# A transformer block on one core: product 6's results are added in two groups, GpSimd subtracts U from another sum, and the last stores are queued earlier

## The chip, the core and the metric

The kernel runs on one core of a Trainium2 chip. The time is the device time of one execution in microseconds (us); three executions are shown, and their median counts. Besides the times there is one profiled execution with its trace. Its engines are called PE (TensorE, matmuls; PEld is its loading of weights), DVE (VectorE), ACT (ScalarE), POOL (GpSimd) and SP (SyncE, which here only issues DMAs). Each engine works through its instructions in the order in which the program gave them to it. POOL cannot read PSUM, the memory into which matmuls write; DVE and ACT can.

## What is computed

One layer on 512 tokens of width 2048: attention of two kinds and a convolution, an output projection, and then a feed-forward part (SwiGLU) with 5632 hidden channels. The change touches only the feed-forward part:

```
h2 = _rms_norm(x, norm2_g[l])
x = x + (jax.nn.silu(h2 @ w_gate[l]) * (h2 @ w_up[l])) @ w_down[l]
```

## The kernel before

**Seven products for eight.** In the feed-forward part every matrix product is cut into 2x2 quarters and computed with seven products of quarters instead of eight (a scheme of Strassen's kind). Each product adds its result to, or subtracts it from, one or more of four sums, which are called (i, k) with i and k 0 or 1; each sum is held in two tiles, a = 0 and a = 1, of 128 x 512. The products come in the order 7, 1, 4, 6, 5, 2, 3 (`ORDER`). Product 7 goes into (1,1), 1 into (0,0), 4 into (1,0), 6 is added to (0,1) and subtracted from (1,0) and (1,1), 5 is subtracted from (1,1), 2 goes into (0,0) and 3 into (0,1). The banks are started anew in products 7, 1, 5 and 2; in 4, 6 and 3 the matmuls go on adding to what the banks hold from the product before the last. So the bank that product 6 leaves holds a term named U, which goes into three sums.

**Up and Down.** `Up` computes gate and up weights, in 11 blocks of two halves each; a half is one pass through the seven products. `Down` computes the down weights in 12 blocks d0 to d11. A Down block covers one of six ranges of pairs of hidden tiles, 4, 3, 4, 3, 4 and 4 pairs long (`RANGES`), and one of two groups g of output channels. The blocks of the ranges with three pairs are d2, d3, d6 and d7. d10 is the last block of g = 1, d11 the last of all, of g = 0.

**Units.** Each product takes two units of weights, c = 0 (A) and c = 1 (B). A unit is a tile of 128 x 1024, two pairs, and in the ranges of three pairs the second unit has one pair, 128 x 512. A weight is used as a high and a low part, so every product of two tiles is three matmuls: high by high, high weight by low activation, low weight by high activation. The high part, `wh`, and a copy of it in PSUM, `wn` (`near` in the code), are made by ACT (L268, L269), and the low part, `wl`, by DVE (L270), which subtracts `wn` from the raw weight. A unit is split two units before it is used (`SPLIT_AHEAD`). The raw weight tiles are called 11, 12, 21, 22 and s, with A or B for the unit; product 7 uses s, 1 uses 11, 4 uses 22, 6 uses 11, 5 uses 21, 2 uses 12 and 3 uses 11 again, which POOL has added to other raw tiles in between (L171).

**The order of the work.** Two lists order what goes along with the matmuls. `evacs` runs ahead of each unit, `extras` behind it, one entry of each per unit: `later(n, ...)` puts a call into entry n, counted from the next run on, so `later(0, ...)` means one unit later. Ahead of each unit stand, in this order, POOL's additions of raw weights, the entry of `evacs`, and the splitting of the unit two ahead. A product writes two of four banks, one for each a, and the product after the next writes the same two again. When a product has been issued it queues `done`, so its banks are read in the first unit of the next product. Product 6 is thus evacuated at the first unit of product 5, ahead of the splitting of 12A; at the second unit 12B is split; at the first unit of product 2 product 5's banks are read and 11A is split.

In Up, `done` reads each of product 6's banks three times on DVE (L1221 to L1223; in the first half ACT makes the first copy for a = 0). In Down (L1455 to L1460), ACT copies each bank into a slot `u` (L1457), POOL subtracts that from (1,1) one or two units later (L1458, done at L1442, the line that every addition in Down has), and DVE subtracts the bank from (1,0) and adds it to (0,1). Product 5 is subtracted from (1,1) by DVE.

**The end.** The sums of Down are turned back with DVE transpositions (`turn_back`, L1349) into buffers `z` and stored by `put` (L1359), four DMAs on SP for each pair of tiles (i, k). In d10 `done` of product 3 queues the eight transpositions and four stores of g = 1 (L1476 to L1480); they run along with d11. The order is (0,0), (1,1), (1,0), (0,1). In d11, which has `self.end`, (1,0) and (1,1) are turned back after products 6 and 5 (L1472 to L1475), and the last product, 3, has a tail of its own (`if tail`): both units are taken first, with no entry of `extras` run; then (0,0) is stored, half of (0,1), and the other half of (0,1), turned on PE, is stored from tiles `end` (L1419). What is left in `evacs` and `extras` runs after that (L1486).

Of the kernel before, what the change touches and what calls it, by code (L numbers as in the profile page):

```python
# [115 lines left out]
def kernel(ctx: ExitStack, tc: tile.TileContext, xT, wi, wo, wgu, wd, cst_in, outT):  # L116
    nc = tc.nc
# [19 lines left out]
    def slot(name, dt=F32, cols=T):  # L137
        return sp.tile([P, cols], dt, name=name, tag="s")

    def bank(name, cols=T, pool="banks"):  # L140
        return psum[pool].tile([P, cols], F32, name=name, tag="b")
# [187 lines left out]
    b = bank("idle")  # L329
    for i in range(WARM):  # L330
        nc.tensor.matmul(b, idle, idle[:, None, :].to_broadcast([P, NT, P]), start=True, stop=True)
    b = idle = None
# [146 lines left out]
    def project(name):  # L479
        b = bank(name, pool="tiles")  # L480
        for half in range(2):
            wh, wl = next_unit()
            for kk in range(8):
                k = 8 * half + kk
                s = slice(kk * P, (kk + 1) * P)
                mm3(b, wh[:, s], wl[:, s], h_hi[k], h_lo[k], k == 0, k == KT - 1)
                if kk == 3:
                    lows_now()
                if kk % 2 == 1:
                    ticks.tick()  # L490
        return b
# [445 lines left out]
    for name in PROJ[HEAD4:]:  # L937
# [4 lines left out]
        b = project(name)  # L942
# [17 lines left out]
    b = box = boxes = shared = None  # L960
# [81 lines left out]
    for half in range(2):  # L1042
        for i, n in enumerate(OUT_ORDER[half]):
            if half == 1 and i == 2:
                open_banks(banks=2, high=2)
            b = bank(f"o{half}_{n}", pool="tiles")
            wh, wl = next_unit()
            for kk in range(8):
                k = 8 * half + kk
# [18 lines left out]
    b = m_hi = m_lo = r1b = mult_a = bias_a = bias_c = over = upper = None  # L1068
# [17 lines left out]
    evacs, extras = [], []  # L1086
# [15 lines left out]
    def later(n, fn, *args, queue=evacs):  # L1102
        while len(queue) <= n:
            queue.append([])
        queue[n].append((fn, *args))
# [59 lines left out]
    class Up:  # L1165
# [39 lines left out]
        def less(self, k, a, b):  # L1205
            t = self.c[1, k, a]
            nc.vector.tensor_sub(t, t, b)

        def done(self, first, q, banks):
            if first and q == 7:  # L1210
                self.c = {}
            by = self.keep if first else self.add
            for a, b in enumerate(banks):
                if q == 7:
                    by(1, 1, a, b)
                elif q == 1:
                    by(0, 0, a, b)
                elif q == 4:
                    by(1, 0, a, b)
                elif q == 6:  # L1220
                    by(0, 1, a, b)  # L1221
                    self.less(0, a, b)
                    self.less(1, a, b)  # L1223
                elif q == 5:
                    self.less(1, a, b)
                else:
                    self.add(0, q - 2, a, b)
            if first:
                return
            if q in (6, 5):  # L1230
                later(1, self.gate, 6 - q, queue=extras)
            elif q == 2:
                self.dram = tc.dram_tile([T, T], F32, name=f"bd{self.n}")
            if q in (2, 3):
                later(0, self.weigh, q - 2)
                later(2, self.turn, q - 2)
                later(3, self.store, q - 2, queue=extras)
            if q == 3:
                first, every = (34, 20) if self.n == NBLOCKS - 1 else (5, 13)
                for at in range(2):  # L1240
                    later(first + every * at, Pair, self.dram, 2 * self.n + at, at, queue=extras)
# [120 lines left out]
    class Down:  # L1362
# [81 lines left out]
        def less(self, i, k, a, src, eng=nc.vector):  # L1444
            self.add(i, k, a, src, eng, "tensor_sub")

        def done(self, q, banks):
            for a, b in enumerate(banks):
                if q == 7:
                    self.add(1, 1, a, b)  # L1450
                elif q == 1:
                    self.add(0, 0, a, b)
                elif q == 4:
                    self.add(1, 0, a, b)
                elif q == 6:  # L1455
                    u = slot(f"d{self.t}u{a}")
                    nc.scalar.copy(u, b)  # L1457
                    later(a, self.less, 1, 1, a, u, nc.gpsimd)  # L1458
                    self.less(1, 0, a, b)
                    self.add(0, 1, a, b)  # L1460
                elif q == 5:
                    self.less(1, 1, a, b)
                    if self.end:
                        self.add(0, 1, a, b)
                elif q == 2 and self.end:

                    t = slot(f"last{a}")
                    nc.scalar.copy(t, b)
                    self.add(0, 0, a, t, nc.gpsimd)
                else:  # L1470
                    self.add(0, q - 2, a, b)
            if self.end and q in (6, 5):  # L1472
                for a in range(2):
                    later(a, turn_back, self.sum(1, int(q == 5), a))
                later(2, put, self.g, 1, int(q == 5))  # L1475
            if q == 3 and self.final:  # L1476
                for n, (i, k) in enumerate(((0, 0), (1, 1), (1, 0), (0, 1))):
                    for a in range(2):
                        later(4 + 2 * n + a, turn_back, self.sum(i, k, a))
                    later(2 * n + 6, put, self.g, i, k, queue=extras)  # L1480

    for t in range(len(DOWN)):
        blk = Down(t)
# [87 lines left out]
```

## Time and profile before

| | |
|---|---|
| median of three executions | 1861.2 us (1860.76 to 1861.59) |
| the profiled execution's own time | 1860.95 us |
| its span, from its first to its last instruction | 1859.2 us |
| PE busy | 1842.0 us, 99% of the span |
| DVE, ACT, POOL busy | 77%, 71%, 55% |
| mean granted PE clock | 0.998 |

The rows of the profile are read like this. In the timeline: start in us from the span's beginning, duration, engine, line, operation, output<-inputs, shapes, count; in brackets the idle time of the engine before it and what ended that. Several alike in a row are merged, with their count. In the view of waits: who waited, for whom, us in total, times, longest. In the groups of DMA issues: count, size of one, median us from issue to landing. The releaser of a wait is inferred; a row that names an engine which had been done long before means another one.

### The profile page before, as it was taken

How to read it: one execution, taken by the hardware profiler on the slowest of the kernel's cores; microseconds unless marked ns; L12 is line 12 of the kernel's file. 1: busy time of each engine (PE TensorE's matmuls, PEld its weight loads, DVE VectorE, ACT ScalarE, POOL GpSimd, SP SyncE). 2: the span in 40 equal slices, each digit the busy share in tenths (PEclk: the TensorE clock that was granted, in tenths of full speed). 3: DMA queues.
4: the chain of work that ended last, by engine and by line, in shares of the span. 5: the costliest groups of instructions: out<-in, count | busy, mean ns of one | idle time of the engine just before them, and what ended most of it. 6: DMA issues, size and time to landing. Idle time of an engine off the chain costs nothing.

```text
span 1859.2 us, 26562 instructions
## 1 busy us (share of the span) xinstructions
PE 1842.0 (99%) x8370; PEld 1526.1 (82%) x8370; DVE 1434.4 (77%) x2054; ACT 1320.6 (71%) x1794; POOL 1013.9 (55%) x778
## 2 busy tenths in 40 slices
PE   9999999999999999999999999999999999999997
PEld 7888888888888888888888888888887887888886
DVE  6778878998689777777777777777777777777776
ACT  6355644553468778888888888878877877877774
POOL 0135533110003567776778768868768658755552
PEclk9999999999999999999999999999999999999999
DMA  7242243333343366777767876777689768767545
GB/s 274 76 147 90 77 139 105 95 123 128 131 136 107 110 163 178 209 213 179 221 185 195 222 192 192 210 191 216 177 263 314 254 210 277 249 217 237 175 141 91
DMA packets 382987, 330.36 MB, mean 178 GB/s; under 512 B 171648, under 2 KB 311552, under 8 KB 382848
## 3 DMA queue, kind: packets, MB, share of 16 engines
q1 hardware_dynamic: 382704, 328.66, 59.8%
q8 instruction: 67, 1.10, 0.2%
q14 instruction: 72, 0.59, 0.1%
q10 hardware_dynamic: 144, 0.01, 0.0%
HBM read 255.56 MB, written 64.63 MB: 172 GB/s over the span
## 4 chain that ended last, share of the span: by engine, by line
PE 95%; DVE 1%; POOL 1%; ACT 1%; issue 1%; DMA 1%; SPq 0%; DVEq 0%; ACTq 0%; POOLq 0%
PE out L1183 15%; PE out L1181 15%; PE out L1184 15%; PE out L1433 6%; PE out L1434 6%; PE out L1432 6%; PE o L309 3%; PE o L307 3%; PE o L308 3%; PE cq L307 2%; PE cq L308 2%; PE cq L309 2%; PE ak L307 1%; PE aq L307 1%; PE av L307 1%
## 5 line engine op out<-in xcount | busy, mean ns | idle before, releaser
L1183 PE MATMUL out<-wl,h 128*128 128x512 f32 x1232 | 479.4, 389 | 0.5 <-DVE wl L270 0.5
L1181 PE MATMUL out<-wh,h 128*128 128x512 f32 x1232 | 479.4, 389 | 0.0
L1184 PE MATMUL out<-wh,h 128*128 128x512 f32 x1232 | 479.3, 389 | 0.0
L1183 PEld LDWEIGHTS out<-wl,h 128*128 128x128 f32 x1232 | 231.2, 188 | 49.0 <-DVE wl L270 0.9
L1184 PEld LDWEIGHTS out<-wh,h 128*128 128x128 f32 x1232 | 231.2, 188 | 48.1
L1181 PEld LDWEIGHTS out<-wh,h 128*128 128x128 f32 x1232 | 231.2, 188 | 47.8
L1433 PE MATMUL out<-wl,a 128*128 128x512 f32 x620 | 241.4, 389 | 5.3 <-DVE wl L270 5.3
L1434 PE MATMUL out<-wh,a 128*128 128x512 f32 x620 | 240.5, 388 | 0.0
L1432 PE MATMUL out<-wh,a 128*128 128x512 f32 x620 | 240.4, 388 | 0.0
L274 ACT CAST wh<-w 128x1024 fp32r<-128x1024 f32 (+2 forms) x94 | 96.8, 1031 | 153.6 <-PE o L308 64.5
L1442 DVE TENSOR_TENSOR y<-y,out 128x512 f32<-128x512 f32 x190 | 126.4, 684 | 65.6 <-PE out L1434 39.0
L252 DVE TENSOR_TENSOR wl<-w,wh 128x1024 fp32r<-128x1024 f32 (+2 forms) x95 | 113.3, 1192 | 41.7 <-ACT wh L274 40.1
L1433 PEld LDWEIGHTS out<-wl,a 128*128 128x128 f32 x620 | 116.4, 188 | 32.6 <-DVE wl L270 8.7
L1432 PEld LDWEIGHTS out<-wh,a 128*128 128x128 f32 x620 | 116.4, 188 | 24.1 <-ACT wh L269 0.2
L1434 PEld LDWEIGHTS out<-wh,a 128*128 128x128 f32 x620 | 116.4, 188 | 23.5
L518 DVE SCALAR_TENSOR_TENSOR y<-bu,cst,y 128x511 f32<-128x511 f32 (+14 forms) x120 | 89.8, 748 | 0.7
L307 PE MATMUL o<-mh_c,wh 128*128 128x512 f32 x128 | 51.1, 399 | 0.0
L307 PE MATMUL cq<-hh,wh 128*128 128x512 f32 x128 | 50.5, 395 | 0.0
L309 PE MATMUL o<-mh_c,wl 128*128 128x512 f32 x128 | 50.0, 391 | 0.0
L308 PE MATMUL cq<-hl,wh 128*128 128x512 f32 x128 | 49.9, 390 | 0.0
L308 PE MATMUL o<-ml_c,wh 128*128 128x512 f32 x128 | 49.9, 390 | 0.0
L309 PE MATMUL cq<-hh,wl 128*128 128x512 f32 x128 | 49.9, 390 | 0.0
(2364 smaller groups left out, 4771.6 us busy)
## 6 DMA issues: line engine op xcount, KB each, us to landing
od<-a SPq DMA_DIRECT2D x154, 256.0 KB, 4.4
a<-od SPq DMA_DIRECT2D x154, 256.0 KB, 5.7
w<-in_wi SPq DMA_DIRECT2D x58, 512.0 KB, 3.4
w<-in_wo SPq DMA_DIRECT2D x32, 512.0 KB, 3.3
x<-in_xT SPq DMA_DIRECT2D x16, 256.0 KB, 7.0
xr<-in_xT SPq DMA_DIRECT2D x16, 256.0 KB, 3.7
x2d<-xr SPq DMA_DIRECT2D x16, 256.0 KB, 2.0
z<-x2d SPq DMA_DIRECT2D x64, 64.0 KB, 3.9
```

The lines of the kernel that those rows point to most:

```text
L252: fn(*args)
L274: (nc.vector.tensor_copy if u == 0 else nc.scalar.copy)(hi[:, :n], t[:, :n])
L307: nc.tensor.matmul(out, wh, xh, start=start, stop=False)
L308: nc.tensor.matmul(out, wh, xl, start=False, stop=False)
L309: nc.tensor.matmul(out, wl, xh, start=False, stop=stop)
L1181: nc.tensor.matmul(b, x[:, high], wh[:, s], start=c == f == 0 and q in (7, 1, 5, 2), stop=False, skip_group_check=True)
L1183: nc.tensor.matmul(b, x[:, high], wl[:, s], start=False, stop=False, skip_group_check=True)
L1184: nc.tensor.matmul(b, x[:, low], wh[:, s], start=False, stop=c == f == 1, skip_group_check=True)
L1432: nc.tensor.matmul(b[:, lo:hi], x[:, high], wh[:, s], start=start, stop=False, skip_group_check=True)
L1433: nc.tensor.matmul(b[:, lo:hi], x[:, high], wl[:, s], start=False, stop=False, skip_group_check=True)
L1434: nc.tensor.matmul(b[:, lo:hi], x[:, low], wh[:, s], start=False, stop=last, skip_group_check=True)
L1442: getattr(eng, op)(t, t, src)
```

## The change

- In Up, product 6's three operations on the bank a = 1 are queued one unit later than those on a = 0 (`six`).
- In Down the same, and their content is arranged anew. DVE subtracts the bank from (1,1) and adds it to (0,1). In d11 DVE also subtracts it from (1,0); elsewhere ACT copies the bank into `u` after that, and POOL subtracts `u` from (1,0) one unit later.
- In d11 the store of (1,0) is queued in `extras`, at the same entry number, and that of (1,1) one entry of `evacs` earlier.
- In d10 the transpositions and stores of g = 1 are queued in earlier entries: the transpositions of a = 0 at 2, 3, 6, 7 instead of 4, 6, 8, 10, and the stores at 4, 5, 8, 9 instead of 6, 8, 10, 12.

```diff
+        def six(self, by, a, b):
+            by(0, 1, a, b)
+            self.less(0, a, b)
+            self.less(1, a, b)
+
...
                 elif q == 6:
-                    by(0, 1, a, b)
-                    self.less(0, a, b)
-                    self.less(1, a, b)
+                    if a:
+                        later(0, self.six, by, a, b)
+                    else:
+                        self.six(by, a, b)
...
+        def six(self, a, b):
+            self.less(1, 1, a, b)
+            self.add(0, 1, a, b)
+            if self.end:
+                self.less(1, 0, a, b)
+            else:
+                u = slot(f"d{self.t}u{a}")
+                nc.scalar.copy(u, b)
+                later(0, self.less, 1, 0, a, u, nc.gpsimd)
+
...
                 elif q == 6:
-                    u = slot(f"d{self.t}u{a}")
-                    nc.scalar.copy(u, b)
-                    later(a, self.less, 1, 1, a, u, nc.gpsimd)
-                    self.less(1, 0, a, b)
-                    self.add(0, 1, a, b)
+                    if a:
+                        later(0, self.six, a, b)
+                    else:
+                        self.six(a, b)
...
             if self.end and q in (6, 5):
                 for a in range(2):
                     later(a, turn_back, self.sum(1, int(q == 5), a))
-                later(2, put, self.g, 1, int(q == 5))
+                later(2 if q == 6 else 1, put, self.g, 1, int(q == 5), queue=extras if q == 6 else evacs)
             if q == 3 and self.final:
                 for n, (i, k) in enumerate(((0, 0), (1, 1), (1, 0), (0, 1))):
                     for a in range(2):
-                        later(4 + 2 * n + a, turn_back, self.sum(i, k, a))
-                    later(2 * n + 6, put, self.g, i, k, queue=extras)
+                        later((2, 3, 6, 7)[n] + a, turn_back, self.sum(i, k, a))
+                    later((4, 5, 8, 9)[n], put, self.g, i, k, queue=extras)
```

## The prediction

> **What bounds the kernel.** I read the page first, then who waited for whom on PE, then the order of time around those waits, then the queue of stores at the end.
>
> ```profile
> span 1859.2 us, 26562 instructions
> ...
> PE 1842.0 (99%) x8370; PEld 1526.1 (82%) x8370; DVE 1434.4 (77%) x2054; ACT 1320.6 (71%) x1794; POOL 1013.9 (55%) x778
> ```
>
> PE is the bound: its matmuls are untouched by the change, so no more can be won than the 17 us (1859.2 - 1842.0) in which it isn't busy. The waits of PE over the whole run, and then of 1500 to 1700 us alone:
>
> ```profile
> PE out L1433 <- DVE wl L270: 5.3, 6, 1.4
> ...
> PE out L1183 <- DVE wl L270: 0.5, 1, 0.5
> ```
> ```profile
> PE out L1433 <- DVE wl L270: 4.3, 4, 1.4
> ```
>
> PE waits for nothing but wl, the low part of a split weight block. Four of the waits lie in 1500 to 1700 us: one in each of the four blocks of three pairs (d2, d3, d6, d7); the two others are in d0. The wait in d6, on PE:
>
> ```profile
> 1659.68 0.39 PE L1434 MATMUL out<-wh,a 128*128 128x512 f32 x1
> 1659.91 0.39 PE L1432 MATMUL out<-wh,a 128*128 128x512 f32 x1
> 1661.27 0.50 PE L1433 MATMUL out<-wl,a 128*128 128x512 f32 x1 [0.97 <-DVE wl L270]
> 1661.61 0.40 PE L1434 MATMUL out<-wh,a 128*128 128x512 f32 x1
> ```
>
> Matmuls start every 0.23 us, so this one came 1.13 us late (1.36 - 0.23), and the next lost another 0.11 (0.34 - 0.23). The profile books only 0.97, because it lets a matmul end 0.39 us after its start. The four waits thus cost about 4.3 + 4 x 0.16 + 4 x 0.11 = 5.4 us. What made wl late, on the other engines:
>
> ```profile
> 1651.27 1.27 ACT L1457 COPY d6u<-out 128x512 f32<-128x512 f32 x2
> 1651.89 2.48 DVE L1442 TENSOR_TENSOR y<-y,out 128x512 f32<-128x512 f32 x4 [0.77 <-ACT d6u L1457]
> ...
> 1652.43 1.02 ACT L268 CAST wn<-w('12', 'd6A')_15933 128x1024 fp32r<-128x1024 f32 x1
> ...
> 1654.28 1.22 DVE L270 TENSOR_TENSOR wl<-w('12', 'd6A')_15933,wn 128x1024 fp32r<-128x1024 f32 x1
> 1654.33 0.59 ACT L268 CAST wn<-w('12', 'd6B')_15955 128x512 fp32r<-128x512 f32 x1
> 1654.85 0.62 ACT L269 CAST wh<-w('12', 'd6B')_15955 128x512 fp32r<-128x512 f32 x1
> 1655.41 0.68 DVE L270 TENSOR_TENSOR wl<-w('12', 'd6B')_15955,wn 128x512 fp32r<-128x512 f32 x1
> ...
> 1656.01 0.68 DVE L1442 TENSOR_TENSOR y<-y,out 128x512 f32<-128x512 f32 x1
> 1656.54 1.05 ACT L269 CAST wh<-w('11', 'd6A')_15783 128x1024 fp32r<-128x1024 f32 x1
> ...
> 1658.08 1.28 POOL L1442 TENSOR_TENSOR y<-y,d6u 128x512 f32<-128x512 f32 x1
> ...
> 1659.40 0.69 DVE L1442 TENSOR_TENSOR y<-y,out 128x512 f32<-128x512 f32 x1 [2.70 <-PE out L1434]
> 1660.00 1.21 DVE L270 TENSOR_TENSOR wl<-w('11', 'd6A')_15783,wn 128x1024 fp32r<-128x1024 f32 x1
> ```
>
> DVE stood idle for 2.70 us before product 5's second subtraction. The row names PE, but product 5 had ended 18 matmuls before 1659.91, at 1655.8; what ended at 1659.36 is POOL's subtraction of U from the same sum, (1,1). DVE works in order, so wl of 11A, wanted by PE from 1660.1, stood behind it. Over the run:
>
> ```profile
> DVE y L1442 <- POOL y L1442: 15.5, 8, 2.7
> ```
>
> **The change, part by part.** *Down, which sum POOL subtracts from.* DVE now takes product 6 from (1,1) itself, and POOL takes U from (1,0), which nobody touches for the next fourteen products. POOL still does two operations a block, DVE four, ACT two copies: no work is added, and DVE's wait for POOL goes.
>
> That doesn't yet free PE, because the order is new. ACT's copy of a bank now follows DVE's two operations on it, and the second bank comes one unit later, behind wl of 12A. Do the two readers of one bank wait for each other? In the fence above DVE began at 1651.89, when the copy begun at 1651.27 had run its 0.6 us; over the run DVE so waited in all twelve blocks:
>
> ```profile
> who waited for it (us, times):
> ...
>   DVE y L1442: 10.0, 12
> ```
>
> I take the reverse order to wait as well, though no row here has it. The Trainium skill (PSUM — Partial Sum Buffer, "PSUM bank collisions raise a hardware error") says that two engines must not be in one bank at once, reads against reads included. By that rule the copy has to wait; without it, the sum would be that of the first rival below, so the rule speaks against the change.
>
> d6 again, with these durations (successors on an engine start 0.1 before the end shown, a hand-over costs 0.04). Bank 0 is complete at 1651.25: DVE's two operations 1651.29 to 1652.58, copy to 1653.21, near of 12A 1653.11 to 1654.13, wl of 12A 1654.17 to 1655.39 (0.1 earlier than before). Behind it bank 1's two, 1655.30 to 1656.59; copy to 1657.21; near and wh of 12B to 1657.70 and 1658.25; wl of 12B to 1658.42; product 5's two operations, no longer waiting, to 1659.62; wl of 11A 1659.53 to 1660.75, before 1661.21. **So wl comes 0.46 earlier where 1.13 was wanted.** What is late next is wh of 11A (near from 1658.18, wh to 1660.2 against PE at 1659.91). Bank 1 is free at 1657.25; product 2 wants it at about 1657.2 (1659.91 less twelve matmuls), so there is no margin there, and I cost it at 0 to 0.1. Three blocks give 0.46; in d3 the wait was 1.4 instead of 1.0 because DVE's start hung on a late copy, and it now leads, so 0.9. **Sum 2.3 us**, between 0 (hand-overs longer than 0.04) and 5.4 (no wait between readers). Blocks of four pairs have 1.4 us more in product 5 and in product 2 each, and of DVE's work nothing more but 0.5 in the second unit; their covers hold. The two waits in d0, 1.0 booked (5.3 - 4.3), I leave as they are; they are neither in the sum nor in its bounds, and would add up to that if the new order took them too.
>
> *Up, product 6's six operations in two groups of three.* The one wait of PE (0.5 booked, about 0.8 by spacing as above) is here:
>
> ```profile
> 1405.38 0.75 DVE L1203 SCALAR_TENSOR_TENSOR b10c<-out,n2r,b10c 128x512 f32<-128x512 f32 x1
> ...
> 1407.23 0.75 DVE L1203 SCALAR_TENSOR_TENSOR b10c<-out,n2r,b10c 128x512 f32<-128x512 f32 x1
> 1407.89 1.28 DVE L1207 TENSOR_TENSOR b10c<-b10c,out 128x512 f32<-128x512 f32 x2
> 1409.08 1.22 DVE L270 TENSOR_TENSOR wl<-w('12', 'u21A')_13542,wn 128x1024 fp32r<-128x1024 f32 x1
> ```
>
> wl of 12A moves up from 1409.08 to 1407.23, so the wait goes; bank 1's three then end about 1410.4 instead of 1409.2, and the gate on ACT with them. Between 0.8 (kept) and 0 (the DMA-fed start of Down eats it) I take 0.4. The other 21 half-blocks show no wait of PE, hence nothing to win.
>
> *The end.* g = 1's eight transpositions move from runs 5 to 12 of the last block to runs 3 to 9. Its last store was queued in extras at 12, but the tail's units run no extras, so it went out last of all:
>
> ```profile
> 1844.91 7.61 SPq L1359 DMA_DIRECT2D out_T<-z  x12
> 1852.62 0.88 SPq L1419 DMA_DIRECT2D out_T<-end  x2
> 1853.56 2.33 SPq L1359 DMA_DIRECT2D out_T<-z  x4
> ```
> ```profile
> out_T<-z SPq DMA_DIRECT2D x4, 128.0 KB, 2.8
> out_T<-end SPq DMA_DIRECT2D x2, 128.0 KB, 1.8
> ```
>
> The last four issues end at 1855.9 and the last begins some 0.6 earlier, so it lands near 1858.1, 1.1 before the span's end. Without them the last is end's second, issued about 1853.1, landing near 1854.9: **3.2 us**. Those four issues and their 512 KB move to run 9, about 1834, where SP waits for DVE. The rest of SP's row is one backlog from 1844.91, so what starts it counts. That is DVE:
>
> ```profile
> 1830.56 2.64 DVE L1442 TENSOR_TENSOR y<-y,out 128x512 f32<-128x512 f32 x4 [0.31 <-ACT d11u L1457]
> ...
> 1837.79 2.44 DVE L1442 TENSOR_TENSOR y<-y,out 128x512 f32<-128x512 f32 x4
> 1840.15 1.21 DVE L270 TENSOR_TENSOR wl<-w('11', 'd11A')_17315,wn 128x1024 fp32r<-128x1024 f32 x1
> ...
> 1842.49 1.18 DVE L270 TENSOR_TENSOR wl<-w('11', 'd11B')_17338,wn 128x1024 fp32r<-128x1024 f32 x1
> 1843.60 1.88 DVE L1349 STREAM_TRANSPOSE z<-y 128x512 f32<-128x512 f32 x3
> ```
>
> In the last block DVE takes two operations from POOL (+1.2 us) and one transposition of run 8 to 11 moves ahead (three of g = 1 there instead of four, -0.6). So wl of 11A ends 0.6 later, at 1842.0, and wl of 11B, with one transposition fewer ahead of it, again at 1843.7. The tail's first wl is wanted no earlier than 1842.2: hidden, by 0.2; if that cover goes, PE loses up to 0.4. At 1843.60 the first transposition is now (1,1)'s own, so its store starts 0.6 before 1844.91. **3.2 + 0.6 = 3.8 us**, between 2.6 (0.6 lost instead) and 5.8 (SP never late: end's copies are done by 1850.1, the two issues begin at once, 2.0 more).
>
> **Sum:** 2.3 + 0.4 + 3.8 = 6.5 us off the profiled execution's 1860.95, which has 1.75 around its span of 1859.2. The median shown is 1861.2, 0.25 above it: **1854.7**.
>
> **Rivals.** *Readers don't wait for each other.* Then ACT copies at once, wl of 11A in d6 is early, and all 5.4 go: 1854.7 - 3.1 = 1851.6. For it: I have no row of a copy behind DVE. Against: the twelve waits of the other order.
>
> *The waits only move.* Hand-overs cost as much as POOL's wait did, Down's start eats the 0.8, the last block loses its 0.2 of cover: 2.6 left, 1858.6, which a measurement can hardly tell from no change (0.2% is 3.7 us). For it: margins of 0 to 0.2 in d6 and the last block.
>
> *Slower: 12A's near copy is late.* Bank 1's operations now stand behind wl of 12A, and that waits for ACT:
>
> ```profile
> DVE wl L270 <- ACT wn L268: 70.3, 89, 3.4
> ```
>
> In the three-pair blocks every us of such lateness goes to PE; from 6.5 / 4 = 1.6 us in each it decides. With the longest wait, 3.4, in all four: 1854.7 + 13.6 = 1868.3. Against: near of 12A started right behind the copies in d6. Up has about 3 us of margin (8.2 from bank 0's end to product 2's second bank, 36 matmuls, against 5.0 of DVE's work).
>
> *It doesn't do what it says* can't be: (1,0) gets nothing after product 6, so the new subtraction can't be waited for.
>
> **Numbers.** Forecast 64%, readers parallel 16%, waits only move 11%, slower 9%. The range 1850.8 to 1858.0 takes in the first two and leaves most of the others, two in ten, out. Faster by over 0.2%, 0.81; within, 0.11; slower, 0.08.
>
> **What will show it.** DVE's wait for POOL on y vanishes; PE's wait for wl in 1500 to 1700 us falls from 4.3 to about 2, and in the three-pair blocks stands behind wh and wl of 11A; L1183's wait is gone; SP's last row is end's two, and the span ends near 1853. Wrong it would be if DVE waits for 12A's near copy in these blocks, or if PE waits for a bank in product 2.

## The result, and the profile after

The changed kernel takes 1853.23 us (median of six executions, 1851.97 to 1854.6), beside 1861.09 us for the kernel before in the same series (six, 1859.25 to 1861.59): a ratio of 0.996 with a 95% interval of 0.9947 to 0.9973. The forecast was 1854.7 us. The profiled execution took 1853.5 us, 7.4 less than the 1860.95 of before; the sum forecast for it was 6.5.

The page of the changed kernel, span and busy time:

```profile
span 1851.8 us, 26509 instructions
## 1 busy us (share of the span) xinstructions
PE 1842.3 (99%) x8370; PEld 1525.9 (82%) x8370; DVE 1436.4 (78%) x2056; ACT 1317.2 (71%) x1792; POOL 1012.6 (55%) x776
```

PE looks as busy as before (1842.0), though its work is the same and the span 7.4 us shorter. That is the modelled end of a matmul: a start up to 0.16 us late is booked as busy, as the prediction noted, and behind a late start even more (in the rows of d6 below 0.37 us stand without a bracket, since the matmul before is shown 0.50 us long). The view of PE's waits in the changed kernel must be read with that in mind:

```profile
PE idle L331 <- DVE ones L341: 1.1, 1, 1.1
PE in L307 <- ACT wh L274: 0.7, 1, 0.7
PE sides L1403 <- DVE y L1417: 0.7, 1, 0.7
PE out L1438 <- ACT wh L269: 0.5, 2, 0.2
PE out L1438 <- ACT d0u L1460: 0.3, 1, 0.3
```

The waits for `wl` (5.3 and 0.5 before) are gone from this list, where the prediction had about 2 us of them left in the three-pair blocks. The three-pair blocks have not become free of waits, though; the pieces are only too small for it. The timeline of PE in d6 of the changed kernel:

```profile
1654.64 0.39 PE L1440 MATMUL out<-wh,a 128*128 128x512 f32 x1
1654.89 0.50 PE L1438 MATMUL out<-wh,a 128*128 128x512 f32 x1
1655.23 0.40 PE L1439 MATMUL out<-wl,a 128*128 128x512 f32 x1
...
1657.52 0.39 PE L1440 MATMUL out<-wh,a 128*128 128x512 f32 x1
1657.83 0.50 PE L1438 MATMUL out<-wh,a 128*128 128x512 f32 x1
1658.43 0.50 PE L1439 MATMUL out<-wl,a 128*128 128x512 f32 x1
1658.77 0.39 PE L1440 MATMUL out<-wh,a 128*128 128x512 f32 x1
```

Against a spacing of 0.227 us, product 2's first matmul into the second bank (1654.89) comes 0.02 late and the one after it 0.11; in product 3, `wh` of 11A costs 0.08 (1657.83), `wl` 0.37 (1658.43), and the matmul behind it 0.11. That is about 0.7 us a block, where before it was 1.25. DVE in the same block of the changed kernel:

```profile
1648.95 1.28 DVE L1448 TENSOR_TENSOR y<-y,out 128x512 f32<-128x512 f32 x2
1651.80 1.22 DVE L270 TENSOR_TENSOR wl<-w('12', 'd6A')_15933,wn 128x1024 fp32r<-128x1024 f32 x1 [1.57 <-ACT wn L268]
1652.94 1.28 DVE L1448 TENSOR_TENSOR y<-y,out 128x512 f32<-128x512 f32 x2
1655.36 0.69 DVE L270 TENSOR_TENSOR wl<-w('12', 'd6B')_15955,wn 128x512 fp32r<-128x512 f32 x1 [1.15 <-ACT wn L268]
1655.97 1.28 DVE L1448 TENSOR_TENSOR y<-y,out 128x512 f32<-128x512 f32 x2
1657.16 1.21 DVE L270 TENSOR_TENSOR wl<-w('11', 'd6A')_15783,wn 128x1024 fp32r<-128x1024 f32 x1
```

And ACT:

```profile
1650.27 0.59 ACT L1460 COPY d6u<-out 128x512 f32<-128x512 f32 x1 [1.32 <-DVE y L1448]
1650.75 1.02 ACT L268 CAST wn<-w('12', 'd6A')_15933 128x1024 fp32r<-128x1024 f32 x1
...
1654.25 0.59 ACT L1460 COPY d6u<-out 128x512 f32<-128x512 f32 x1 [1.50 <-DVE y L1448]
1654.74 0.60 ACT L268 CAST wn<-w('12', 'd6B')_15955 128x512 fp32r<-128x512 f32 x1
```

Product 5's two subtractions now run in one piece (1655.97, x2): DVE no longer waits for POOL. In its place ACT waits for DVE at each bank, 1.32 and 1.50 us, and DVE then waits for ACT's near copy, 1.57 and 1.15. DVE's waits of that kind over the run grew from 70.3 us (89 times) to this, in the changed kernel:

```profile
DVE wl L270 <- ACT wn L268: 95.2, 111, 2.6
```

SP at the end, in the changed kernel:

```profile
1816.01 32.42 SPq L1365 DMA_DIRECT2D out_T<-z  x32
1848.53 0.89 SPq L1425 DMA_DIRECT2D out_T<-end  x2
```

The four stores that stood behind `end` (2.33 us from 1853.56) are gone from there; `end` goes out last, and the span ends 3.3 us after 1848.53, where before it ended 6.6 us after `end`'s first issue (1852.62). The first of these rows merges stores with idle time between them; from 1840.95 on they follow each other without a pause.

**Where the time went.** Worked out from the whole trace: each matmul's start that comes later than 0.227 us after the one before, summed by block; the tail is the time from the last matmul's start to the end of the span. The experiments below stand in the same table. The last block, d11, has 0.3 or none, but 0.9 in e1; the other Down blocks that are not named have none. All times in us.

| kernel | Up | d0 | d2 | d3 | d6 | d7 | tail | span |
|---|---|---|---|---|---|---|---|---|
| before | 0.86 | 1.58 | 1.25 | 1.76 | 1.25 | 1.25 | 9.82 | 1859.2 |
| changed | 0.10 | 1.41 | 0.68 | 0.68 | 0.68 | 0.68 | 6.11 | 1851.8 |
| e1, end undone | 0.10 | 0.00 | 0.68 | 0.64 | 0.68 | 0.64 | 9.34 | 1854.6 |
| e2, Up undone | 0.94 | 0.69 | 0.68 | 0.65 | 0.64 | 0.68 | 6.17 | 1852.0 |
| e3, Down undone | 0.10 | 1.84 | 1.27 | 1.75 | 1.26 | 1.26 | 5.34 | 1854.1 |
| e4, copy first | 0.10 | 1.16 | 0 | 0 | 0 | 0 | 5.98 | 1848.6 |
| e5, swap alone | 0.10 | 0.88 | 0 | 0.11 | 0 | 0 | 10.15 | 1852.7 |
| e6, e4 with `end` on ACT | 0.10 | 0.00 | 0 | 0 | 0 | 0 | 14.95 | 1856.5 |
| e7, end alone | 0.10 | 0.99 | 1.27 | 1.76 | 1.26 | 1.26 | 5.75 | 1853.6 |
| e8, e6 with stores of `z` on ACT | 0.10 | 1.39 | 0 | 0 | 0 | 0 | 12.75 | 1856.8 |
| e9, changed again | 0.10 | 1.81 | 0.69 | 0.73 | 0.68 | 0.71 | 6.41 | 1852.8 |
| e10, e4 again | 0.10 | 1.82 | 0 | 0 | 0 | 0 | 6.51 | 1850.4 |
| e11, no groups | 0.10 | 0.17 | 0 | 0.11 | 0 | 0 | 6.24 | 1847.3 |
| e12, e10 with Up in one group | 0.10 | 2.29 | 0 | 0 | 0 | 0 | 6.51 | 1851.2 |

From before to changed: 2.79 us less in the three-pair blocks (5.51 to 2.72), 0.76 in Up, 0.17 in d0, 3.71 in the tail. Together that is 7.43, the 7.4 us of the span.

The column of d0 is made of three parts. In product 3 the kernels in which POOL subtracts from (1,1), before, e3 and e7, lose 0.7 us each, and no other kernel does: there DVE stood behind POOL as in the three-pair blocks. The row of before:

```profile
1453.69 0.69 DVE L1442 TENSOR_TENSOR y<-y,out 128x512 f32<-128x512 f32 x1 [2.63 <-POOL y L1442]
```

In product 2 the changed kernel and e9 lose 1.1 us, e2 0.7, and no kernel in which the copy goes first loses more than 0.05; e1, which has the changed order too, loses nothing there. What is left is product 4's wait, from 0 to 2.3 us, to which e12 comes back.

### The profile page after: what moved, and what is told of

Read it like the earlier page. It is cut to its first block, busy times and chain, and to the rows that moved or that the text cites. A ratio compares the mean times of both kernels' runs of the same rounds, so it can differ in the third digit from the quotient of the medians.

```text
span 1851.8 us, 26509 instructions
## 1 busy us (share of the span) xinstructions
PE 1842.3 (99%) x8370; PEld 1525.9 (82%) x8370; DVE 1436.4 (78%) x2056; ACT 1317.2 (71%) x1792; POOL 1012.6 (55%) x776
## 3 DMA queue, kind: packets, MB, share of 16 engines
q8 instruction: 66, 1.08, 0.2%
## 4 chain that ended last, share of the span: by engine, by line
PE 97%; DVE 1%; issue 1%; DMA 1%; ACT 1%; POOL 0%; SPq 0%; DVEq 0%; ACTq 0%; POOLq 0%
PE out L1181 15%; PE out L1184 15%; PE out L1183 15%; PE out L1439 7%; PE out L1438 7%; PE out L1440 7%; PE o L309 3%; PE o L307 3%; PE o L308 3%; PE cq L307 2%; PE cq L308 2%; PE cq L309 2%; PE ak L307 1%; PE aq L307 1%; PE av L307 1%; PE aq L309 1%
```

## The experiments

The theory: the swap of sums takes POOL off DVE's path, but ACT's copy, put behind DVE's two operations at the bank, takes half of that back; the end is a matter of what SP issues last. The rivals: the two groups do it, or the bank's readers do not matter; at the end, the gain comes from work moved away from the last matmuls. Every kernel was timed beside the kernel before on the same chip; the latter's medians were 1860.55 (e1 to e4), 1860.64 (e5 to e8), 1860.8 (e9 to e11) and 1860.57 us (e12).

**e1: the changed kernel with the end as before.**

```diff
-                later(2 if q == 6 else 1, put, self.g, 1, int(q == 5), queue=extras if q == 6 else evacs)
+                later(2, put, self.g, 1, int(q == 5))
...
-                        later((2, 3, 6, 7)[n] + a, turn_back, self.sum(i, k, a))
-                    later((4, 5, 8, 9)[n], put, self.g, i, k, queue=extras)
+                        later(4 + 2 * n + a, turn_back, self.sum(i, k, a))
+                    later(2 * n + 6, put, self.g, i, k, queue=extras)
```

> The changed kernel with the end put back: g = 1's transpositions and stores at their old entries, the stores of (1,0) and (1,1) too; Up and Down as changed. My theory (the end is worth 3.7 us by itself, since four stores came last of all): the span goes from 1851.8 to 1855.5, SP's last row is again four stores behind end's two, and PE's last matmul stays within 0.4 us of 1845.7. Rival (the stores came earlier only because PE ended earlier): the span stays at 1851.8 to 1852.3.

Measured: 1858.36 us, ratio 0.9987 (0.9977 to 0.9996). SP's queue in e1:

```profile
1834.65 13.49 SPq L1365 DMA_DIRECT2D out_T<-z  x17
1848.24 0.88 SPq L1425 DMA_DIRECT2D out_T<-end  x2
1849.18 2.34 SPq L1365 DMA_DIRECT2D out_T<-z  x4
```

The four stores are back behind `end`, and the tail is 3.2 us longer than in the changed kernel (9.34 - 6.11); 3.1 of it lie behind `end`'s first issue (6.4 us to the end of the span instead of 3.3), which is what the prediction priced these stores at. PE also lost 0.9 us (0.6 booked) in the last block, where the changed kernel loses 0.3: `wl` of 11B stands behind two transpositions there, in the changed kernel behind one. The profiled execution (1856.33) is the shortest of e1's ten and has no waits in d0, so its span lies below what its median stands for.

**e2: the changed kernel with Up's product 6 in one group.**

```diff
                 elif q == 6:
-                    if a:
-                        later(0, self.six, by, a, b)
-                    else:
-                        self.six(by, a, b)
+                    by(0, 1, a, b)
+                    self.less(0, a, b)
+                    self.less(1, a, b)
```

> The changed kernel with Up's product 6 in one group of six again. My theory: the wait of PE at 1410 us comes back (0.8 by the matmuls' spacing), the start of Down takes none of it: span 1852.6. Rival (Down's start, fed by DMAs, eats it): the wait comes back, the span stays at 1851.8 within 0.2.

Measured: 1854.84 us, ratio 0.9967 (0.9955 to 0.9979), which overlaps the changed kernel's interval; by medians it is 1.4 to 1.6 us slower. Of Up's 0.94 in the table, 0.10 stands at the start of Up in every kernel, and only 0.35 at 1410 us, where before has 0.76; 0.49 stands in another half-block, at 915 us, in which no other kernel waits. d0 has 0.69 instead of 1.41, and the span is only 0.2 us longer, but this profiled execution is the shortest of e2's six. The span fits the rival, the medians rather the theory; e12 asks again.

**e3: the changed kernel with Down as before.**

```diff
                 elif q == 6:
-                    if a:
-                        later(0, self.six, a, b)
-                    else:
-                        self.six(a, b)
+                    u = slot(f"d{self.t}u{a}")
+                    nc.scalar.copy(u, b)
+                    later(a, self.less, 1, 1, a, u, nc.gpsimd)
+                    self.less(1, 0, a, b)
+                    self.add(0, 1, a, b)
```

> The changed kernel with Down's product 6 as before: POOL subtracts U from (1,1), one group, in d11 too. My theory: in d2, d3, d6 and d7 PE waits again for wl of 11A, 1.1 to 1.5 us by spacing instead of 0.7, so the span grows by 2.7 to 1854.5; DVE waits for POOL on y again, some 15 us. Rival (Down's new order is worth nothing, its waits only moved): 1851.8 to 1852.3.

Measured: 1855.75 us, ratio 0.9975 (0.9965 to 0.9985). The waits of DVE and of PE in e3:

```profile
DVE y L1448 <- POOL y L1448: 15.5, 8, 2.7
```
```profile
PE out L1439 <- DVE wl L270: 5.6, 6, 1.4
```

Both are those of before to within 0.3 us. So Down's edit alone removes them. The span grows by 2.3 us, less than the 2.8 in the blocks and 0.4 in d0, since the tail is 0.8 shorter. In e3 POOL again has two operations of d11 that the change gave to DVE; e11, which also has them on POOL, has a tail of 6.24, so they are not shown to be the reason.

**e4: the changed kernel with ACT's copy ahead of DVE's two operations in Down.**

```diff
         def six(self, a, b):
+            if not self.end:
+                u = slot(f"d{self.t}u{a}")
+                nc.scalar.copy(u, b)
+                later(0, self.less, 1, 0, a, u, nc.gpsimd)
             self.less(1, 1, a, b)
...
-            else:
-                u = slot(f"d{self.t}u{a}")
-                nc.scalar.copy(u, b)
-                later(0, self.less, 1, 0, a, u, nc.gpsimd)
```

> The changed kernel with one thing moved: in Down ACT copies each of product 6's banks ahead of DVE's two operations on it, not behind them. My theory (what is left of the waits comes from ACT standing behind DVE at the bank): ACT's copy waits for DVE in no block, near of 12A starts about 1.3 us earlier against the bank's end, the waits of PE in the four three-pair blocks (0.7 each by spacing) vanish and those in d0 shrink: span 1848.3 to 1849.3. Rival (the two groups are what keeps the rest, since bank 1's work stands behind wl of 12A): the waits stay, span 1851.5 to 1852.

Measured: 1850.93 us, ratio 0.995 (0.9935 to 0.9964). ACT in d6 of e4:

```profile
1647.40 0.59 ACT L1456 COPY d6u<-out 128x512 f32<-128x512 f32 x1
1647.89 1.02 ACT L268 CAST wn<-w('12', 'd6A')_15933 128x1024 fp32r<-128x1024 f32 x1
```

And DVE:

```profile
1648.03 1.28 DVE L1448 TENSOR_TENSOR y<-y,out 128x512 f32<-128x512 f32 x2 [0.77 <-ACT d6u L1456]
1649.23 1.21 DVE L270 TENSOR_TENSOR wl<-w('12', 'd6A')_15933,wn 128x1024 fp32r<-128x1024 f32 x1
...
1653.40 1.22 DVE L270 TENSOR_TENSOR wl<-w('11', 'd6A')_15783,wn 128x1024 fp32r<-128x1024 f32 x1
```

Now DVE waits 0.77 us, ACT does not wait, the near copy is done by 1648.91, and `wl` of 12A starts in one piece behind DVE's two. From the first bank's handling (copy 1647.40) to the end of `wl` of 11A pass 7.2 us; in the changed kernel it was 9.4 (1648.95 to 1658.37). PE has no wait in the three-pair blocks, d0's in product 2 is gone as well (product 4's stands, 1.1 us), and PE's busy time falls by 2.7 us, about what the late starts came to that had been booked as work:

```profile
PE 1839.6 (100%) x8370; PEld 1526.7 (83%) x8370; DVE 1438.3 (78%) x2056; ACT 1318.5 (71%) x1792; POOL 1011.8 (55%) x776
```

**e5: the kernel before with the swap of sums alone, in one group, the copy first as it was.**

```diff
                     nc.scalar.copy(u, b)
-                    later(a, self.less, 1, 1, a, u, nc.gpsimd)
-                    self.less(1, 0, a, b)
+                    if self.end:
+                        later(a, self.less, 1, 1, a, u, nc.gpsimd)
+                        self.less(1, 0, a, b)
+                    else:
+                        later(a, self.less, 1, 0, a, u, nc.gpsimd)
+                        self.less(1, 1, a, b)
                     self.add(0, 1, a, b)
```

> The kernel before with one thing changed: in d0 to d10 POOL subtracts U from (1,0) and DVE subtracts the bank from (1,1). Two groups, Up and the end are as before. My theory (DVE's wait for POOL is the whole cause of the waits in the three-pair blocks, and grouping isn't needed for it): DVE waits for POOL on y nowhere, PE's waits in 1500 to 1700 us, 5.4 us by spacing, vanish, span 1859.2 - 5.4 = 1853.8. Rival (product 6's four operations in a row make wl late by themselves): waits of at least 0.5 each stay, span 1856 or more.

Measured: 1854.48 us, ratio 0.9968 (0.9956 to 0.9979): 6.2 us under the kernel before, without groups and without the end. PE's waits in all of e5 for the sums' lines:

```profile
PE out L1433 <- DVE wl L270: 0.5, 1, 0.5
```

That one is in d0, in product 4. The swap takes 5.4 of the 5.51 us in the three-pair blocks and the 0.7 of d0's product 3, so Down's two groups are not needed for it. The span, 1852.7, lies 1.1 under the theory's, since Up's wait was not there either.

**e6: e4 with the last two stores issued by ACT.**

```diff
-                    nc.sync.dma_start(outT.rearrange("n p t -> (n p) t")[to:to + P, TH:], last[c].rearrange("p b a j -> p (b a j)"))
+                    nc.scalar.dma_start(outT.rearrange("n p t -> (n p) t")[to:to + P, TH:], last[c].rearrange("p b a j -> p (b a j)"))
```

> e4 with end's two stores issued by ACT instead of SP. My theory (the end is set by SP's backlog of issues): end's stores are issued when the copies are done, some 2 us earlier, the last landing is that of (0,1)'s half, near 1846.9 on the clock of e4, so the span goes from 1848.6 to 1847.7. Rival (the DMA engines themselves set the end, issuing earlier only shares them): 1848.4 to 1848.8.

Measured: 1858.81 us, ratio 0.9992 (0.9983 to 1.0001). Theory and rival both fall: by medians it is 7.9 us slower than e4, and its tail is 9.0 us longer. The waits of SP's queue in the last 32 us of e6, and ACT's issue there:

```profile
SPq L1365 <- DMA out_T<-end: 15.0, 1, 15.0
```
```profile
1842.36 0.83 ACTq L1425 DMA_DIRECT2D out_T<-end  x2
```

SP stood still for 15 us until a store had landed that ACT issued only at 1842.36; then it had sixteen stores of `z` still to issue. In the trace the DMAs of both queues take eight completion semaphores in turn, and each is held until the one before it on its semaphore has landed: SP's next store went out at 1844.15, and ACT's first store, which has the same semaphore, had landed at 1844.09. On SP alone that order was the queue's own; with `end` on ACT, a store that SP could have issued early stood behind one that ACT issues last.

The Trainium skill (Perfetto Trace Analysis, "DMA Optimizations") says that balancing DMAs over the engines that can issue them may help where the generation of descriptors is the bottleneck. Here, with these shared semaphores, it did the opposite: SP stood still for those 15.0 us.

**e7: the kernel before with the end's edits alone** (the diff of e1 the other way, in the kernel before).

> The kernel before with the end's edits alone (g = 1's transpositions and stores earlier, (1,0)'s and (1,1)'s stores requeued). My theory: the waits in Up and Down stay as they were, PE's last matmul stays within 0.4 us of 1849.4, and the span falls by 3.2 for the store that came last and 0.3 to 0.6 for the earlier start of SP's backlog: 1855.5. Rival (the end's gain needs PE's): 1858 or more.

Measured: 1855.7 us, ratio 0.9978 (0.9968 to 0.9987), 4.9 us under the kernel before. The tail is 4.1 us shorter (9.82 to 5.75). The span lost 1.5 more than that, about 1.35 of it where no code differs: Up's wait was not there (0.76) and d0 had 0.59 less, in product 4. SP's queue in e7:

```profile
1834.92 15.25 SPq L1359 DMA_DIRECT2D out_T<-z  x18
1850.27 0.88 SPq L1419 DMA_DIRECT2D out_T<-end  x2
```

**e8: e6 with half of the tail's stores of z on ACT as well.**

```diff
-                        put(self.g, 0, 0)
+                        put(self.g, 0, 0, engs=(nc.sync, nc.scalar))
...
-                        put(self.g, 0, 1, 0, TH)
+                        put(self.g, 0, 1, 0, TH, engs=(nc.sync, nc.scalar))
```

> e6 with the last two stores from z, (0,0) and the half of (0,1), issued by SP and ACT in turn, two DMAs each. My theory: with the backlog shared, (0,1)'s half is issued about 1.5 us earlier; 1.0 MB in these last stores at some 180 GB/s is 5.6 us from 1840.6 on e4's clock, so nothing can land before 1846.2: span 1847.0 to 1847.5. Rival (ACT's copies of end stand behind its DMAs and come late): 1848 or more.

Measured: 1857.41 us, ratio 0.9984 (0.9974 to 0.9993). The expectation fell in the same way: SP's queue waited 13.8 us, now for a store of `z`.

```profile
SPq L1365 <- DMA out_T<-z: 13.8, 1, 13.8
```

**e9, e10 and e11: the changed kernel again, e4 again, and the kernel before with swap and end together** (the diffs of e5 and e7; neither Up nor Down in two groups), side by side on one chip.

> The changed kernel itself, beside the next two on one chip. Its waits in d0 differed between the runs so far (1.3 us by spacing more in its first profile than in e1, with the same code up to there). My theory (that part follows when DMAs land, not the change): the three-pair blocks show 0.7 us each again, d0's waits may differ by about 1 us; time 1852 to 1855. Rival (d0's waits belong to the new order): they stand as in the first profile, within 0.2.

> e4 again. My theory: 2.5 to 3.5 us under e9, none of PE's waits in d2, d3, d6 and d7, so it is the fastest of all. Rival (e4's gain was a matter of the chip or of d0): within 1 us of e9.

> The kernel before with e5's swap and the end's edits together, product 6 in one group in Up and in Down. My theory (in Down the two groups bring nothing that the swap with the copy ahead doesn't): no waits in d2, d3, d6, d7, and only Up's 0.8 is lost against e10, so it stands 0 to 1 us over e10, span 1848.6 to 1849.8. Rival (the groups carry part of Down's gain): 1.5 us or more over e10.

Measured: e9 1853.43 us, ratio 0.9961 (0.9948 to 0.9975); e10 1850.77, 0.9947 (0.9935 to 0.996); e11 1848.99, 0.9936 (0.9924 to 0.9949). Putting the copy first again brings 2.7 us. e11 is the fastest of all, 4.4 us under the changed kernel; it had been expected at or a little over e10, and that missed by 1.8. The profiles tell the two apart mainly by d0, 0.17 against 1.82, and by a wait of 1.0 us in e10's attention part, where no code differs. e9's d0 answers its expectation by halves: product 2's 1.1 us stand as in the first profile, so they go with the new order, though e1 escapes them; product 4's differ (0.25 and 0.67). PE's waits in e11 are down to these two:

```profile
PE idle L331 <- DVE ones L341: 1.1, 1, 1.1
PE sides L1397 <- DVE y L1411: 0.7, 1, 0.7
```

**e12: e10 with Up in one group** (the diff of e2), to see whether the groups in Up make d0's wait.

> e10 with Up's product 6 in one group; what then differs from e11 is Down's two groups alone. My theory (e10's 1.7 us of wait in d0, which e11 lacks, follows when DMAs land and is not made by Up's groups): d0's wait is somewhere from 0 to 1.7 us, the time 1848.5 to 1851.5, and no wait of PE in d2, d3, d6 and d7. Rival 1 (Up's groups, by delaying the gate, make d0 wait): d0 waits 0.2 or less, the time is e11's within 0.7. Rival 2 (Down's groups make it): d0 waits 1 us or more.

Measured: 1850.66 us, ratio 0.9944 (0.993 to 0.9959), like e10. d0's wait is 2.29, over what was expected; so Up's groups don't make it. Down's groups, rival 2, would fit the number, but can't make it directly: the wait is for `wl` of 22B, in product 4, and the first product 6 of Down comes after that; and e1 and e6, which have Down's groups, have no wait there. DVE in e12:

```profile
1434.66 0.71 DVE L1266 STREAM_TRANSPOSE b10c<-b10c 128x512 f32<-128x512 f32 x1 [3.72 <-POOL b10c L1262]
1435.91 0.71 DVE L1266 STREAM_TRANSPOSE b10c<-b10c 128x512 f32<-128x512 f32 x1 [0.53 <-POOL b10c L1262]
1436.54 1.18 DVE L270 TENSOR_TENSOR wl<-w('22', 'd0B')_13908,wn 128x1024 fp32r<-128x1024 f32 x1
```

And POOL in e12:

```profile
1426.26 2.42 POOL L171 TENSOR_TENSOR w('21', 'd0A')_13648<-w('21', 'd0A')_13648,w('22', 'd0A')_13878 128x1024 f32<-128x1024 f32 x1 [2.21 <-DMA w('22', 'd0A')_13878<-in_wd]
...
1433.34 2.53 POOL L1262 TENSOR_TENSOR b10c<-b10c,b10c 128x512 f32<-128x512 f32 x2
```

`wl` stands behind the last transpositions of Up, those behind POOL's two operations on the same tile, and those behind an addition of raw weights that waits for a load of 22A. In e11 it is the same, but sooner; POOL there:

```profile
1422.70 2.42 POOL L171 TENSOR_TENSOR w('21', 'd0A')_13648<-w('21', 'd0A')_13648,w('22', 'd0A')_13878 128x1024 f32<-128x1024 f32 x1 [1.95 <-DMA w('22', 'd0A')_13878<-in_wd]
...
1429.75 2.55 POOL L1257 TENSOR_TENSOR b10c<-b10c,b10c 128x512 f32<-128x512 f32 x2
```

The addition is 3.56 us earlier in e11, and PE finds `wl` all but ready. In all fourteen profiles this `wl` starts 10.3 us after the addition, and the addition 0.13 us after the load has landed; the wait goes with how long after d0's first matmul `wl` starts: none at 11.1 us (e1) and 11.4 (e6), 0.2 at 12.6 (e11), 1.8 at 14.3 (e10), 2.3 at 14.8 (e12). So d0's wait in product 4 follows the landing of that load. Why SP issues that load later in some executions stays open, and with it whether e11's lead over e10 and e12 is due to its code; their intervals overlap.

## Why the prediction was right

**The swap of sums.** DVE's wait for POOL went, as forecast, and e3 and e5 show the edit alone to take and bring it. The two operations, copy, near copy and `wl` followed each other as worked out: from DVE's start at the first bank to the end of `wl` of 11A the prediction has 9.46 us (1651.29 to 1660.75), the trace 9.42. A block's waits fell by 0.57 us instead of 0.46, d3's by 1.08 instead of 0.9, so the step gave 2.8 us where 2.3 were forecast; by medians, e3 puts Down's edit at 2.3 to 2.5 us (1855.75 against 1853.23 and 1853.43).

**The readers of one bank.** The choice on which the sum hung, that ACT's copy waits behind DVE, is what ACT's rows show (1.32 and 1.50 us), and e4 removes it for 2.3 to 2.7 us by medians. The first rival, 1851.6, had the right size for a kernel in which nothing waits there, but not for this one.

By the rule of the Trainium skill that the prediction named (PSUM — Partial Sum Buffer, "PSUM bank collisions raise a hardware error"), the trace agrees: the program keeps the two engines apart in this order (1.32 and 1.50 us) as it does in the other (0.77 us in e4).

**Late next.** `wh` and `wl` of 11A, as forecast (0.08 and 0.37). The second bank in product 2 had its margin of nothing (0.02 late). In d0, however, it was later: PE waited there for ACT's copy, 0.3 us booked and 0.54 by spacing, and then 0.57 for `wh` of 12B. That was named as a sign of error, and it is one for the sentence that the covers of the four-pair blocks hold: in d0 they didn't. Nor did d0's two waits of before stay, as the prediction left them: the one in product 3 was DVE's wait for POOL again, and the swap took its 0.70; the one in product 4 was shorter by 0.56 because a load landed sooner. That 1.1 more and 1.3 less nearly cancel, so that the sum shows nothing of it, is luck; over the fourteen profiles d0's waits run from 0 to 2.29.

**Up.** 0.76 us in the profile instead of 0.4: a term mis-sized by half in that execution. But the wait is one that comes and goes: with one group it stands in two of the six profiles in the table (before, and e2 with 0.35), with two groups in none of eight. e12 without the groups is as fast as e10 with them (1850.66 and 1850.77). The groups in Up were not shown to be worth anything.

**The end.** 3.7 us in the tail, 3.8 forecast. From `end`'s first issue to the end of the span it is 3.3 us less than before (6.6 to 3.3), where the four stores were worked out at 3.2; `end` itself goes out 0.4 sooner after the last matmul (2.9 us instead of 3.3), where 0.6 was expected. PE shows no wait for the tail's `wl` of 11A, so its cover held; the 0.3 us in d11 are for `wl` of 11B, before and after. By medians the end's edits bring more, 4.9 us (e7) and 4.9 to 5.1 (e1 against e9 and the first series). The prediction's bounds of 2.6 to 5.8 hold it; what beyond the tail makes it is open.

**The rivals on the other side.** "The waits only move" (1858.6) falls with the three-pair blocks' 2.79 us. "12A's near copy is late" (1868.3) needed lateness of more than 1.6 us beyond the chain; DVE's longest wait for a near copy shrank from 3.4 to 2.6, and in d6 its 1.57 is the chain as worked out.

**Readings that were off without moving the sum.** The view of PE's waits also had `PE idle L331` (1.1) and `PE sides L1397` (0.7), which the changed kernel has too, so `wl` was not all that PE waited for. The 17 us in which PE is not booked as busy were no ceiling: in e4 its busy time is 1839.6 us for the same matmuls. (1,0) is not left alone for fourteen products everywhere: d1 and d2 have the same group, and there product 4 comes back to it six products later. And DVE's wait for 12A's near copy was named as a sign of error, but the prediction's own chain has it (1652.58 to 1654.17, 1.6 us), so the 1.57 measured speaks for the chain.

Of the change as it was made, the swap and the end carry all of the gain that was shown; copying behind DVE gives back 2.3 to 2.7 us. The version that leaves the copy first and makes no groups, e11, beats both kernels: 1848.99 us, ratio 0.9936 (0.9924 to 0.9949).

## What to carry to other kernels

When two engines read one bank, let the one go first whose result feeds the longer chain: here a copy of 0.6 us ahead of two operations of 1.3 us decided 2.3 to 2.7 us of the whole. Give the slow engine the sum that nobody touches next, and queue a store where it surely runs ahead of the last ones. Look at the spacing of matmul starts as well as at the booked waits, since a busy PE can hide a few tenths of a microsecond at each late start.

## What was not expected of the hardware

- A store moved from SP's queue to ACT's held SP up for 15.0 us (e6) and made the kernel 7.9 us slower; in this program the two queues are chained by the completion semaphores that their DMAs share in turn.
- d0's waits differ between executions of the same code up to there, from 0.00 us (e1) to 1.41 (the changed kernel) and 1.81 (e9), in part with the landing of one load; a single profile is not enough to price an edit of 1 us.
